# First loads of a two-layer decoder trunk: x and the first weight chunk on three queues instead of one

## The chip, the cores and the metric

The kernel runs on one core of a Trainium2 chip. The metric is the device time of one execution in microseconds (us); lower is better. The time before is 397.64 us, the median of three runs (397.17 to 398.45).

## What is computed

The reference is a decoder trunk of two layers on one sequence of 256 tokens with 1024 features. Layer 0 is a gated DeltaNet mixer, layer 1 a sparse-attention mixer. Only the head of layer 0 matters here: x is multiplied by a wide input matrix, whose columns give queries, keys, values, a gate and two small logits per head.

```python
def gated_deltanet_mixer(x, w_in, conv_w, a_log, dt_bias, norm_w, w_out):
    b_sz, t_len, _ = x.shape
    proj = x @ w_in
    qkv = jax.nn.silu(causal_short_conv(proj[..., :DN_QKV_WIDTH], conv_w))
    z = proj[..., DN_QKV_WIDTH:DN_QKV_WIDTH + DN_VAL_WIDTH]
    b_logit = proj[..., DN_QKV_WIDTH + DN_VAL_WIDTH:DN_QKV_WIDTH + DN_VAL_WIDTH + DN_HEADS]
    a_logit = proj[..., DN_QKV_WIDTH + DN_VAL_WIDTH + DN_HEADS:]
    ...
    return o.reshape(b_sz, t_len, DN_VAL_WIDTH) @ w_out
```

Everything else (the delta rule, the normalisation, the attention of layer 1, the output projections) comes after and is not touched.

## The kernel before

All arithmetic is in float32, and each large product is made of three matmuls: an operand is split into a high part, a cast to the type `fp32r`, and a low part, the difference to the original. For x these are `xh` and `xl`, for a weight chunk `hi` and `lo`. A product is high by high, low by high and high by low.

**Weights.** They stream from device memory in chunks of 128 x 1024 float32 (512 KB). `load_to` (line 156) issues the loads on the queue of the sync engine (SP) into a ring of five buffers named `raw`. `split_to` (lines 173 to 180) makes the high part on the scalar engine (ACT) and the low part on GpSimd (Pool); for the second chunk alone half of the cast and the low part are done on the vector engine (DVE). A `raw` buffer is free for another load when its low part is done. The order of chunks is the list `order`: 24 of `wqkv` first.

**The opening.** The transposed x, `xT`, is 128 x 8 x 256, 1 MB; it is loaded in four quarters of 256 KB (line 280), two of the eight blocks of 256 columns each. The first weight chunk, `first` (in the trace `raw_first`), is loaded in two halves of 256 KB (line 279). The tuple `FIRST = (1, 2)` puts a half ahead of the second and of the third quarter. All six are issued on SP's queue. The small logit matrix `wba` (64 KB) is loaded on ACT's queue (line 272), after a dummy exponential that brings in ACT's function table (line 269). Two small tables go out on Pool's queue, `sel` (line 288, 4.5 KB) and `nw` (line 290, 0.5 KB); `sel` is read first by `inv_expand`, some twenty chunks later, and `nw` later still.

Then ACT, DVE, Pool and the tensor engine (PE) work by quarters (the loop `for q in range(5)`). ACT casts, in this order: `wbs` from `wba` (line 308), the first quarter (line 333), the first weight half (line 316), the second quarter, the second weight half, and the last two quarters in four pieces. DVE makes `xl` from each (line 334), Pool `lo_first` from each weight half (line 317). PE runs 28 warm-up matmuls on a constant (line 324), then for each of the eight blocks four matmuls, two of the logits `gps` (line 338) and two of the first chunk `ps0` (line 340, `pv` in the trace), and two groups of four with the low weights (lines 343 and 352): 40 in all. The next chunk's matmuls (line 360) follow.

**What sets the order.** The order on PE, ACT, DVE and Pool is the order in which the program is written. SP's is left to a scheduler. Each load counts its completion on one of eight counters (`DMAHW0` to `DMAHW7`) for the queues of SP and ACT together, taken in turn, and on others (`DMASW`) for Pool's; the next load on a counter waits until the one before it has landed.

Of the kernel before, what the change touches and what calls it, by code (L numbers as in the profile page):

```python
# [9 lines left out]
F32 = mybir.dt.float32  # L10
F32R = mybir.dt.float32r
BF16 = mybir.dt.bfloat16
AF = mybir.ActivationFunctionType
# [4 lines left out]
P = 128  # L18
# [17 lines left out]
FIRST = (1, 2)  # L36
# [52 lines left out]
def trunk(ctx: ExitStack, tc: tile.TileContext, I: dict, out: bass.AP):  # L89
    nc = tc.nc  # L90
    V, S, G, PE = nc.vector, nc.scalar, nc.gpsimd, nc.tensor
# [22 lines left out]
    cp = ctx.enter_context(tc.tile_pool(name="cp", bufs=1))  # L114
# [14 lines left out]
    def xtile(tag, name, dt=F32R, shape=(P, 8, T)):  # L129
        return xp_.tile(list(shape), dt, tag=tag, name=name)  # L130
# [4 lines left out]
    def pjb(name):  # L135
        if state["wide"]:
            state["wide"] = 3 - state["wide"]
            if state["wide"] == 1:
# [4 lines left out]
    order = ([("wqkv", i) for i in range(24)] + [("wz", i) for i in range(8)] +  # L143
             [("wo", i) for i in range(8)] + [("skv", i) for i in range(4, 12)] +
             [("skv", i) for i in range(0, 4)] + [("bq", i) for i in range(4)] +
             [("w1", i) for i in range(4)] + [("bq", i) for i in range(4, 8)] +
             [("bz", i) for i in range(24)] + [("bo", i) for i in range(8)])
# [117 lines left out]
    warm = nc.const_aps.tensor(1.0, (P, 256), BF16)  # L265
    ones = cp.tile([P, 1], F32, name="ones")
    V.memset(ones, 1.0)
    tab = cp.tile([P, 1], F32, name="tab")
    S.activation(tab, ones, AF.Exp)
    xT = xtile("x1", "xT", F32)  # L270
    wba = cp.tile([P, 8, 16], F32, name="wba")
    nc.scalar.dma_start(wba, I["wba"])
    first = ring.tile([P, 1024], F32, tag="raw", name="raw_first", bufs=NRAW)
    raws[order[0]] = first
    state["l"] = 1
    for q in range(4):
        if q in FIRST:
            c = slice(FIRST.index(q) * 512, FIRST.index(q) * 512 + 512)
            nc.sync.dma_start(first[:, c], I[order[0][0]][0][:, c])
        nc.sync.dma_start(xT[:, 2 * q:2 * q + 2, :], I["xT"][:, 2 * q:2 * q + 2, :])  # L280
    al = cp.tile([P, 2, NH], F32, name="al")
    load_to(2)
    nc.sync.dma_start(al, I["al"].partition_broadcast(P))
# [1 line left out]
    nc.sync.dma_start(cw, I["cw"])  # L285
    load_to(3)
    sel = cp.tile([P, NSEL], F32, name="sel")
    nc.gpsimd.dma_start(sel, I["ca"])
    nw = cp.tile([P, 1], F32, name="nw")
    nc.gpsimd.dma_start(nw, I["nw"])  # L290
    ident, tri, suf = (cp.tile([P, P], F32, name=nm) for nm in ("ident", "tri", "suf"))
    for m, inc, base, cmp in ((ident, 1, 0, ALU.is_equal), (tri, 1, 0, ALU.is_ge), (suf, -1, 0, ALU.is_gt)):
        G.memset(m, 1.0)
# [10 lines left out]
    def add_pairs(n):  # L304
        G.tensor_tensor(pair[0:2 * n, 0:n], ident[0:2 * n, 0:n], ident[0:2 * n, n:2 * n], op=ALU.add)  # L305

    add_pairs(16)
    S.copy(wbs[:, :, 0:16], wba)
    V.tensor_tensor(wbs[:, :, 16:32], wba, wbs[:, :, 0:16].bitcast(F32), op=ALU.subtract)

    xh = xtile("xh", "xh")
    xl = xtile("xl", "xl")

    def split_first(c):
        h, l = splits[order[0]]
# [11 lines left out]
    for q in range(5):  # L327
        if q < 4:
            c = slice(2 * q, 2 * q + 2)
# [150 lines left out]
    def diag_ap(t):  # L480
        return bass.AP(tensor=t.tensor, offset=t.offset, ap=[[16 * 128 + 16, 128], [128, 16], [1, 16]])
# [77 lines left out]
        return MT1[r, h, c] if t == 0 else MT2[r, h, c]  # L559

    def inv_load():
        nc.sync.dma_start(Bd, diag_ap(scrM))

    def inv_rows(r):
# [111 lines left out]
    def clear():  # L676
# [4 lines left out]
        for t in range(2):  # L681
# [6 lines left out]
             6: [lambda: decay_rows(1), lambda: defer(1, lambda: decay_diff(1)), lambda: defer(1, lambda: decay_exp(0))],  # L688
             9: [lambda: defer(2, lambda: decay_exp(1)), lambda: clear()],
             INV + 1: [lambda: inv_load()],  # L690
             INV + 5: [lambda: inv_store()],
             INV + 7: [lambda: inv_expand()],
# [875 lines left out]
```

## Time and profile before

| | |
|---|---|
| time, median of 3 runs | 397.64 us (397.17 to 398.45) |
| the profiled execution's own time | 398.08 us |
| its span, first to last instruction | 396.1 us |
| mean granted clock of PE | 0.994 |
| PE busy | 383.1 us, 97% |
| ACT, DVE, Pool busy | 55%, 56%, 62% |
| loads and stores | 58.61 MB, mean 148 GB/s |

The page counts an engine as busy while any of its instructions runs. Matmuls overlap: one of 256 columns is shown as 0.28 us long while the next starts 0.12 us later, so a count of matmuls is turned into time with the pitch between starts, not with the length of one. "SPq", "ACTq" and "Pool" rows of the form `DMA_DIRECT2D` are the issue of a load, not its transfer; how long it takes to land is given by the view of the DMA issues. "Idle before <-releaser" in brackets is how long the engine stood idle, and what it was waiting for.

### The profile page before, as it was taken

How to read it: one execution, taken by the hardware profiler on the slowest of the kernel's cores; microseconds unless marked ns; L12 is line 12 of the kernel's file. 1: busy time of each engine (PE TensorE's matmuls, PEld its weight loads, DVE VectorE, ACT ScalarE, POOL GpSimd, SP SyncE). 2: the span in 40 equal slices, each digit the busy share in tenths (PEclk: the TensorE clock that was granted, in tenths of full speed). 3: DMA queues.
4: the chain of work that ended last, by engine and by line, in shares of the span. 5: the costliest groups of instructions: out<-in, count | busy, mean ns of one | idle time of the engine just before them, and what ended most of it. 6: DMA issues, size and time to landing. Idle time of an engine off the chain costs nothing.

```text
span 396.1 us, 7532 instructions
## 1 busy us (share of the span) xinstructions
PE 383.1 (97%) x2868; PEld 339.4 (86%) x2868; DVE 220.5 (56%) x583; ACT 218.6 (55%) x425; POOL 247.2 (62%) x158
## 2 busy tenths in 40 slices
PE   7999999999999999999999999999999999999992
PEld 4999999999989987868999888888888888778891
DVE  1778776668533455454530645645656465577626
ACT  4788666656654372625641658565474647456410
POOL 4699999747454856895872987193644637109051
PEclk9999999999999999999999999999999999999997
DMA  6866679744334314663554664243415243201011
GB/s 220 324 214 204 224 220 294 192 134 162 109 108 151 115 52 163 194 238 101 202 167 161 257 216 158 106 139 123 163 37 177 65 150 108 106 2 53 2 53 53
DMA packets 23475, 58.61 MB, mean 148 GB/s; under 512 B 6672, under 2 KB 9232, under 8 KB 23312
## 3 DMA queue, kind: packets, MB, share of 16 engines
q1 hardware_dynamic: 23232, 58.07, 44.2%
q8 instruction: 22, 0.36, 0.4%
q14 instruction: 13, 0.11, 0.1%
q10 hardware_dynamic: 144, 0.07, 0.1%
q0 software_dynamic: 64, 0.01, 0.0%
HBM read 55.90 MB, written 2.23 MB: 147 GB/s over the span
## 4 chain that ended last, share of the span: by engine, by line
PE 87%; POOL 4%; DVE 4%; DMA 2%; issue 1%; ACT 1%; POOLq 0%; SPq 0%; DVEq 0%; ACTq 0%
PE pbz L228 6%; PE pbz L230 5%; PE pbz L229 5%; PE op L1370 4%; PE s L1299 3%; PE ptp L1341 2%; POOL lo_skv L180 2%; PE pwz L228 2%; PE pk L210 2%; PE pbq L228 2%; PE pq L210 2%; PE pq L212 2%; PE pq L211 2%; PE pk L211 2%; PE pk L212 2%; PE pwz L230 2%
## 5 line engine op out<-in xcount | busy, mean ns | idle before, releaser
L180 POOL TENSOR_TENSOR lo_bz<-raw_bz,hi_bz 128x1024 fp32r<-128x1024 f32 x24 | 56.8, 2393 | 39.4 <-PE pbz L229 18.2
L180 POOL TENSOR_TENSOR lo_wqkv<-raw_wqkv,hi_wqkv 128x1024 fp32r<-128x1024 f32 x22 | 52.5, 2403 | 6.6 <-ACT hi_wqkv L176 4.5
L228 PE MATMUL pbz<-hi_bz,x1h 128*128 128x512 f32 x96 | 38.9, 405 | 0.0
L230 PE MATMUL pbz<-lo_bz,x1h 128*128 128x512 f32 x96 | 37.7, 392 | 0.0
L229 PE MATMUL pbz<-hi_bz,x1l 128*128 128x512 f32 x96 | 37.6, 392 | 0.0
L180 POOL TENSOR_TENSOR lo_bo<-raw_bo,hi_bo 128x1024 fp32r<-128x1024 f32 x8 | 18.9, 2388 | 23.7 <-ACT hi_bo L176 18.7
L180 POOL TENSOR_TENSOR lo_skv<-raw_skv,hi_skv 128x1024 fp32r<-128x1024 f32 x12 | 28.4, 2402 | 4.7 <-PE pskv L230 4.7
L180 POOL TENSOR_TENSOR lo_wz<-raw_wz,hi_wz 128x1024 fp32r<-128x1024 f32 x8 | 19.4, 2444 | 16.9 <-ACT hi_wz L176 16.9
L176 ACT CAST hi_bz<-raw_bz 128x1024 fp32r<-128x1024 f32 x24 | 25.2, 1052 | 4.1 <-POOL pair L305 2.7
L1348 ACT COPY PT<-ptp 128x512 f32<-128x512 f32 x24 | 14.1, 588 | 24.2 <-PE ptp L1341 24.2
L180 POOL TENSOR_TENSOR lo_bq<-raw_bq,hi_bq 128x1024 fp32r<-128x1024 f32 x8 | 19.1, 2397 | 12.6 <-ACT hi_bq L176 12.5
L180 POOL TENSOR_TENSOR lo_wo<-raw_wo,hi_wo 128x1024 fp32r<-128x1024 f32 x8 | 19.0, 2389 | 11.5 <-ACT hi_wo L176 11.5
L176 ACT CAST hi_wqkv<-raw_wqkv 128x1024 fp32r<-128x1024 f32 x22 | 22.8, 1043 | 0.8 <-DMA raw_wqkv<-in_wqkv 0.8
L228 PEld LDWEIGHTS pbz<-hi_bz,x1h 128*128 128x128 f32 x96 | 18.0, 188 | 4.1
L230 PEld LDWEIGHTS pbz<-lo_bz,x1h 128*128 128x128 f32 x96 | 18.0, 188 | 4.0
L229 PEld LDWEIGHTS pbz<-hi_bz,x1l 128*128 128x128 f32 x96 | 18.1, 188 | 2.8
L1332 ACT ACTIVATE pt<-s,mx 128x256 f32<-128x256 f32 x32 | 13.4, 472 | 11.0 <-DVE mx L1315 8.8
L210 PE MATMUL pk<-xh,hi_wqkv 128*128 128x256 f32 x64 | 18.7, 292 | 0.0
L210 PE MATMUL pq<-xh,hi_wqkv 128*128 128x256 f32 x64 | 18.5, 289 | 0.0
L212 PE MATMUL pq<-xh,lo_wqkv 128*128 128x256 f32 x64 | 18.1, 283 | 0.0
L211 PE MATMUL pq<-xl,hi_wqkv 128*128 128x256 f32 x64 | 18.1, 283 | 0.0
L211 PE MATMUL pk<-xl,hi_wqkv 128*128 128x256 f32 x64 | 18.1, 283 | 0.0
(357 smaller groups left out, 1259.1 us busy)
## 6 DMA issues: line engine op xcount, KB each, us to landing
raw_bz<-in_bz SPq DMA_DIRECT2D x24, 512.0 KB, 3.3
raw_wqkv<-in_wqkv SPq DMA_DIRECT2D x23, 512.0 KB, 4.2
raw_skv<-in_skv SPq DMA_DIRECT2D x12, 512.0 KB, 3.3
raw_wz<-in_wz SPq DMA_DIRECT2D x8, 512.0 KB, 3.8
raw_wo<-in_wo SPq DMA_DIRECT2D x8, 512.0 KB, 3.3
raw_bq<-in_bq SPq DMA_DIRECT2D x8, 512.0 KB, 3.5
raw_bo<-in_bo SPq DMA_DIRECT2D x8, 512.0 KB, 3.3
raw_w<-in_w SPq DMA_DIRECT2D x4, 512.0 KB, 3.5
```

The lines of the kernel that those rows point to most:

```text
L176: S.copy(h, r)
L180: e.tensor_tensor(l, r, h.bitcast(F32), op=ALU.subtract)
L210: PE.matmul(ps[:, 0:T], wh[:, kt, :], ah[:, kt, :], start=kt == 0, stop=False)
L211: PE.matmul(ps[:, 0:T], wh[:, kt, :], al_[:, kt, :], start=False, stop=False)
L212: PE.matmul(ps[:, 0:T], wl[:, kt, :], ah[:, kt, :], start=False, stop=kt == 7)
L228: PE.matmul(ps, ah[:, kt, tt], wh[:, k4, cols], start=kt == 0, stop=False)
L229: PE.matmul(ps, al_[:, kt, tt], wh[:, k4, cols], start=False, stop=False)
L230: PE.matmul(ps, ah[:, kt, tt], wl[:, k4, cols], start=False, stop=kt == 7)
L1299: PE.matmul(sp[:, j, 0:n], lq, kk[:, hh // 4, c0:c0 + n], start=i == 0, stop=i == 1)
L1332: S.activation(pt[:, :, b, :], s4[:, :, b, :], AF.Exp, bias=mx[:, b:b + 1])
L1348: S.copy(PT.rearrange("p a b c -> p (a b c)"), TP[u])
L1370: PE.matmul(o3[:, r, 1 + b, :], PT[:, j, b, :], vt_[:, b, j, g_, :], start=j == 0, stop=j == 1)
```

## The change

The six loads of the opening are divided among three queues. SP keeps the first and the third quarter of x. ACT's queue takes, after `wba`, the second quarter and the second weight half. Pool's queue takes the first weight half and the last quarter. The dummy exponential comes after ACT's three issues. `sel` and `nw` leave Pool's queue; they are written in `inv_load`, on SP's queue. The cast of `wba` is written after the allocation of `xh` and `xl` instead of ahead of it, with no other work between.

```diff
-    tab = cp.tile([P, 1], F32, name="tab")
-    S.activation(tab, ones, AF.Exp)
     xT = xtile("x1", "xT", F32)
     wba = cp.tile([P, 8, 16], F32, name="wba")
-    nc.scalar.dma_start(wba, I["wba"])
     first = ring.tile([P, 1024], F32, tag="raw", name="raw_first", bufs=NRAW)
     raws[order[0]] = first
     state["l"] = 1
-    for q in range(4):
-        if q in FIRST:
-            c = slice(FIRST.index(q) * 512, FIRST.index(q) * 512 + 512)
-            nc.sync.dma_start(first[:, c], I[order[0][0]][0][:, c])
-        nc.sync.dma_start(xT[:, 2 * q:2 * q + 2, :], I["xT"][:, 2 * q:2 * q + 2, :])
+
+    def load_x(e, q):
+        e.dma_start(xT[:, 2 * q:2 * q + 2, :], I["xT"][:, 2 * q:2 * q + 2, :])
+
+    def load_first(e, q):
+        c = slice(q * 512, q * 512 + 512)
+        e.dma_start(first[:, c], I[order[0][0]][0][:, c])
+
+
+    load_x(nc.sync, 0)
+    nc.scalar.dma_start(wba, I["wba"])
+    load_first(nc.gpsimd, 0)
+    load_x(nc.scalar, 1)
+    load_x(nc.sync, 2)
+    load_first(nc.scalar, 1)
+    load_x(nc.gpsimd, 3)
+    tab = cp.tile([P, 1], F32, name="tab")
+    S.activation(tab, ones, AF.Exp)
...
     sel = cp.tile([P, NSEL], F32, name="sel")
-    nc.gpsimd.dma_start(sel, I["ca"])
     nw = cp.tile([P, 1], F32, name="nw")
-    nc.gpsimd.dma_start(nw, I["nw"])
...
     def inv_load():
+        nc.sync.dma_start(sel, I["ca"])
+        nc.sync.dma_start(nw, I["nw"])
         nc.sync.dma_start(Bd, diag_ap(scrM))
```

Line numbers after `load_x` are higher in the changed kernel; the four casts of the opening are then lines 318, 340, 323 and 340.

The start of SP's queue before. `raw_wqkv_101` is the second weight chunk, `raw_wqkv_106` the third, 217, 219 and 221 the fourth to the sixth; `al` and `cw` are small tables, and the brackets name the counters and engines waited for:

```order
L280 DMA xT<-in_xT 128x512
L279 DMA raw_first<-in_wqkv 128x512
L280 DMA xT<-in_xT 128x512
L279 DMA raw_first<-in_wqkv 128x512
L280 DMA xT<-in_xT 128x512 x2
L156 DMA raw_wqkv_101<-in_wqkv 128x1024
L283 DMA al<-in_al 128x16 [waits DMAHW0_49]
L285 DMA cw<-in_cw 128x96 [waits DMAHW1_49]
L156 DMA raw_wqkv_106<-in_wqkv 128x1024 [waits DMAHW2_49]
L156 DMA raw_wqkv_217<-in_wqkv 128x1024 [waits DMAHW3_49]
L156 DMA raw_wqkv_219<-in_wqkv 128x1024 [waits DMAHW4_49]
L156 DMA raw_wqkv_221<-in_wqkv 128x1024 [waits DMAHW5_49,Pool_49]
```

The third chunk waits for counter 2, on which the second quarter of x lands. The same place after; here 215, 217 and 219 are the fourth to the sixth chunk, and `pek` and `pev` are two tables of 8 KB:

```order
L275 DMA xT<-in_xT 128x512 x2
L156 DMA raw_wqkv_101<-in_wqkv 128x1024
L293 DMA al<-in_al 128x16
L295 DMA cw<-in_cw 128x96
L156 DMA raw_wqkv_106<-in_wqkv 128x1024 [waits DMAHW0_49]
L156 DMA raw_wqkv_215<-in_wqkv 128x1024 [waits DMAHW1_49]
L156 DMA raw_wqkv_217<-in_wqkv 128x1024 [waits DMAHW2_49]
L569 DMA sel<-in_ca 128x9 [waits DMAHW3_49]
L570 DMA nw<-in_nw 128x1 [waits DMAHW4_49]
L1092 DMA pek<-in_pek 128x16 [waits DMAHW5_49]
L1092 DMA pev<-in_pev 128x16 [waits DMAHW6_49]
L156 DMA raw_wqkv_219<-in_wqkv 128x1024 [waits DMAHW7_49,DMASW0_49,Pool_49]
```

Four of the six x and weight loads have left the queue, the second chunk is its third load instead of its seventh, the third chunk waits for counter 0, on which ACT's `wba` lands, and `sel`, `nw`, `pek` and `pev` stand ahead of the sixth chunk.

The start of ACT's program before, from the table load to the last cast of x:

```order
L269 ACT_TABLE_LOAD
L269 ACTIVATE tab<-ones 128x1 [waits DVE_49]
L272 DMA wba<-in_wba 128x128
L308 CAST wbs<-wba 128x8x16 [waits DMAHW3_49]
L333 CAST xh<-xT 128x512 [waits DMAHW0_49]
L316 CAST hi_first<-raw_first 128x512 [waits DMAHW1_49]
L333 CAST xh<-xT 128x512 [waits DMAHW2_49]
L316 CAST hi_first<-raw_first 128x512 [waits DMAHW4_49]
L333 CAST xh<-xT 128x256 [waits DMAHW5_49]
```

And after:

```order
L283 DMA wba<-in_wba 128x128
L275 DMA xT<-in_xT 128x512
L279 DMA raw_first<-in_wqkv 128x512
L290 ACT_TABLE_LOAD
L290 ACTIVATE tab<-ones 128x1 [waits DVE_49]
L318 CAST wbs<-wba 128x8x16 [waits DMAHW0_49]
L340 CAST xh<-xT 128x512 [waits DMAHW1_49]
L323 CAST hi_first<-raw_first 128x512 [waits DMASW0_49]
L340 CAST xh<-xT 128x512 [waits DMAHW2_49]
L323 CAST hi_first<-raw_first 128x512 [waits DMAHW4_49]
L340 CAST xh<-xT 128x256 [waits DMAHW3_49]
```

Two more issues stand ahead of the table load, and the cast of the first weight half waits for a load of Pool's queue (`DMASW0`). The order of the casts is the same. On Pool, the issues of `raw_first` and `xT` stand where those of `sel` and `nw` stood.

## Rows read from the trace of the kernel before

**Rows 1.** The page's first part: busy us, share of the span, instructions.
```profile
PE 383.1 (97%) x2868; PEld 339.4 (86%) x2868; DVE 220.5 (56%) x583; ACT 218.6 (55%) x425; POOL 247.2 (62%) x158
```

**Rows 2.** Stretches: length, busy PE, PEld, DVE, ACT, POOL (instructions), clock, DMA share, GB/s.
```profile
6.30:14.00 7.70, 5.95 (x44) 4.98 (x44) 4.98 (x8) 4.48 (x9) 2.58 (x2) 1.00 0.95 350
14.00:380.00 366.00, 363.49 (x2735) 322.87 (x2733) 206.50 (x555) 211.47 (x412) 237.06 (x137) 1.00 0.45 147
```

**Rows 3.** The chain that ended last, 0 to 14 us: start, us, what.
```profile
1.71 6.79 DMA xT<-in_xT
8.52 0.63 ACT xh L333
...
13.34 0.47 PE pv L352 x4
```

**Rows 4.** Timeline of PE, 0 to 10 us: start, us, instruction [idle before].
```profile
0.84 5.50 PE L324 MATMUL warm<-const-bfloat16-1.0 128*128 128x256 bf16 x28 [0.84 <-PEq L1558]
...
6.86 0.38 PE L340 MATMUL pv<-xh,hi_first 128*128 128x256 f32 x1 [0.22 <-ACT hi_first L316]
...
9.19 0.31 PE L338 MATMUL gps<-xh,wbs 128*32 128x256 f32 x1 [1.23 <-ACT xh L333]
...
9.91 0.31 PE L338 MATMUL gps<-xl,wbs 128*32 128x256 f32 x1 [0.30 <-DVE xl L334]
```

**Rows 5.** Timeline of DVE, the last two subtracts of x.
```profile
11.38 0.75 DVE L334 TENSOR_TENSOR xl<-xT,xh 128x256 fp32r<-128x256 f32 x2
```

**Rows 6.** Timeline of SP's queue: issues of loads.
```profile
1.24 0.42 SPq L279 DMA_DIRECT2D raw_first<-in_wqkv  x1
...
2.65 0.91 SPq L280 DMA_DIRECT2D xT<-in_xT  x2
...
8.51 0.33 SPq L156 DMA_DIRECT2D raw_wqkv<-in_wqkv  x1
...
11.20 0.33 SPq L156 DMA_DIRECT2D raw_wqkv<-in_wqkv  x1
```

**Rows 7.** DMA issues at 1.24, 3.1 and 11.20: size, us from issue to landing.
```profile
raw_first<-in_wqkv SPq DMA_DIRECT2D x1, 256.0 KB, 4.9
...
xT<-in_xT SPq DMA_DIRECT2D x1, 256.0 KB, 7.4
...
raw_wqkv<-in_wqkv SPq DMA_DIRECT2D x1, 512.0 KB, 5.9
```

**Rows 8.** Stretches of half a microsecond, columns as in rows 2.
```profile
6.00:6.50 0.50, 0.50 (x5) 0.16 (x2) 0.27 (x2) 0.50 (x2) 0.00 (x0) 1.00 0.56 193
8.00:8.50 0.50, 0.00 (x0) 0.00 (x0) 0.00 (x0) 0.00 (x0) 0.17 (x1) 1.00 1.05 414
```

**Rows 9.** Timeline of ACT, 0 to 7 us.
```profile
0.80 1.28 ACT L269 ACT_TABLE_LOAD   x1 [0.80 <-PEq L1558]
...
5.47 0.30 ACT L308 CAST wbs<-wba 128x128 fp32r<-128x128 f32 x1 [3.17 <-DMA wba<-in_wba]
5.67 0.61 ACT L333 CAST xh<-xT 128x512 fp32r<-128x512 f32 x1
6.19 0.61 ACT L316 CAST hi_first<-raw_first 128x512 fp32r<-128x512 f32 x1
```

**Rows 10.** Timeline of POOL: its two issues, and its first weight subtracts.
```profile
1.31 0.78 POOL L288 DMA_DIRECT2D sel<-in_ca  x1 [0.81 <-POOLq L1558]
2.09 0.56 POOL L290 DMA_DIRECT2D nw<-in_nw  x1
...
14.38 9.48 POOL L180 TENSOR_TENSOR lo_wqkv<-raw_wqkv,hi_wqkv 128x1024 fp32r<-128x1024 f32 x4 [3.20 <-ACT hi_wqkv L176]
```

**Rows 11.** DMA issues on POOL's queue, and its packets from 4 to 5 us.
```profile
sel<-in_ca POOLq DMA_DIRECT2D x1, 4.5 KB, 5.0
nw<-in_nw POOLq DMA_DIRECT2D x1, 0.5 KB, 6.2
...
q0 software_dynamic: 17, 0.00, 5.6%
```

More of the change, by code (lines that the diff above doesn't have):

```diff
@@ L307, in trunk @@
     add_pairs(16)
+    xh = xtile("xh", "xh")
+    xl = xtile("xl", "xl")
     S.copy(wbs[:, :, 0:16], wba)
     V.tensor_tensor(wbs[:, :, 16:32], wba, wbs[:, :, 0:16].bitcast(F32), op=ALU.subtract)
-    xh = xtile("xh", "xh")
-    xl = xtile("xl", "xl")
     def split_first(c):
```

## The prediction

> **What bounds the kernel now.** The page's busy times come first: the tensor engine (PE) is busy for 383.1 of 396.1 us [rows 1]. A change that takes no matrix work away can win only where PE stands idle, so the next view is busy time by stretch. From 14 to 380 us PE is idle for 2.5 us in all (366.00 - 363.49) [rows 2]. The change touches none of that; it works on the opening, where PE runs 40 matmuls of real work (the row's 44, less the last warm-up matmul and three of the next chunk). The chain of waits gives their pitch, 0.47 us for four or 0.1175 each, and their end, 13.34 + 0.47 = 13.81 us [rows 3]. Forty of them need 4.7 us. The warm-up matmuls run from 0.84 to 6.34 [rows 4], so the opening takes 13.81 - 6.34 = 7.47 us, and **2.8 us of it are idle**. That is the most that this change can be worth.
>
> Who ends the idle time? The chain says: the load of the second quarter of x, issued at 1.71 and landing 6.79 later at 8.5; then its cast on ACT, its low half on DVE, and PE [rows 3]. PE waits 1.23 us for that cast; the waits behind DVE are short, such as the 0.30 at 9.91 [rows 4]. So the six loads of the opening set the time. All are on SP's queue today: quarter, weight half, quarter, weight half, quarter, quarter. The first weight half, issued at 1.24, landed 4.9 later, at 6.1; the last quarter, the second of the pair from 2.65 and so issued at about 3.1, landed 7.4 later, at 10.5 [rows 6, 7]. From the second quarter (8.5) to the last (10.5) three loads landed, 0.67 us each: that is the pace of one queue once it flows. Before that it did not flow: from 6.0 to 6.5 us the DMA engines were busy 56% at 193 GB/s, from 8.0 to 8.5 fully, at 414 GB/s [rows 8].
>
> **The change part by part.** *The split of the loads.* PE cannot start real work before 6.34, since the warm-up is kept, so the first quarter may land later than today by some tenths (its cast starts at 5.67 [rows 9]) at no cost. PE's second matmul needs the cast of the first weight half. That cast stands in ACT's row behind the first quarter's, and everything behind it on ACT waits with it. From its landing PE needs 0.65 us (0.61 for the cast [rows 9], and the start) and 39 matmuls, 4.6 us. So PE's opening ends no earlier than **landing + 5.25**. Today that floor is 6.1 + 5.25 = 11.4, and the late quarters of x add the other 2.4.
>
> After the change this half is the first load on Pool's queue, in the slot where the small table `sel` is today. That slot starts at 1.31 and takes 0.78 to issue [rows 10], and 4.5 KB issued there landed 5.0 later, at 6.3; the answers by microsecond show packets of its queue only from 4 us on [rows 11]. No row shows a large load on this queue. The bounds: not before 6.3, the landing of a table; not after 8.7, which is 1.31 plus 7.4, the slowest quarter of today. In between, 256 KB at the full pace add 0.67 to 6.3 (7.0), at a third of it 2.0 (8.3), since three queues then share the DMA engines. I take **7.5**, nearer the full pace, because the engines have idle room until 7 us.
>
> The Trainium skill (DMA: Bandwidth & Descriptors, Latency and other measured facts) gives a software-generated queue about 1 us to its first byte and a hardware one about 0.6. By that, an estimate from the page, the half would flow from about 2.5 us and be no later than today, worth some 2 us in the end. The trace disagrees: the packets of `sel` came at least 2.7 us after its issue began.
>
> The other loads: the second quarter becomes the second load of ACT's queue and the third quarter the second of SP's, the place from which the weight half landed at 6.1; with sharing I take 6.5 to 8. The second weight half is third on ACT's queue, as the second quarter is on SP's today (8.5). The last quarter is second on Pool's queue, where `nw` today lands at 2.09 + 6.2 = 8.3 [rows 10, 11]; with bulk in front and beside it I take 9.5 to 10.5, at worst as today. The ACT casts then run at 7.5, 8.0, 8.5 and so on, at the pitch of 0.52 of today's first two (6.19 - 5.67) [rows 9], and reach the last quarter at about 10. Even if it lands at 10.5, its two casts (0.7), DVE's last subtract (0.75 for two, so 0.4 [rows 5]) and six matmuls (0.7) end at 12.3. The weight half therefore rules: 7.5 + 5.25 = 12.75, and 0.2 for waits behind DVE like today's: **12.95 against 13.81, 0.9 us less**.
>
> *ACT's queue.* Two more issues, 0.4 us each by SP's [rows 6], now stand ahead of the table load of 1.28 and the dummy exponential. The table load starts near 2.1 and ends near 3.4, and ACT's next work stands at 5.47, where its small table lands [rows 9]: hidden with almost 2 us to spare. If that table came by 3.5, the 1.3 us would show.
>
> *Pool.* Two issues take the place of two issues; behind them come the masks, and then Pool waits for the cast of the weight half, as today. Nothing.
>
> *SP's queue.* Its order is not written by hand. The two small tables, with two others of 8 KB drawn forward, come to stand ahead of the sixth weight chunk: four issues, about 1.7 us. Today that chunk goes out at 11.20 and lands 5.9 later, at 17.1 [rows 6, 7]; its subtract is the last of the four that Pool runs from 14.38 in 9.48 us, so it starts at 21.5 [rows 10]. A delay of 1.7, and the cast between, fit there. Nothing on PE. In the other direction, the third chunk waits today for the second quarter of x and goes out at 8.51 [rows 6]; in the new order it waits for ACT's table and can go near 5.5. That is no gain, since PE does not wait for it, but it puts 512 KB more beside the last x loads; it is one reason why I leave the last quarter at up to 10.5.
>
> *After the opening.* Every engine's work hangs on PE's progress, and 2.5 us of idle time in 366 leave little that could swallow a shift, so I carry the 0.9 to the end in full. The sum is made against the profiled execution, 398.08, whose span is 396.1: 397.2. The median of the runs, 397.64, lies 0.44 below it, so the forecast is 397.64 - 0.9 = **396.7 us**.
>
> **The rivals.** *All loads come on time.* Three queues fill the idle room of [rows 8], and the weight half lands with the speed of a small table, at 6.3: PE ends at 6.3 + 5.25 + 0.2 = 11.75, a gain of 2.1, 395.6 us. For it: the engines' idle share, and loads that arrive more nearly in the order of use. Against it: that slot needs 5.0 us even for 4.5 KB.
>
> *Nothing moves.* The bytes are the same, the same DMA engines carry them, and the queues interleave: the weight half comes at 13.81 - 5.45 = 8.4 instead of 6.1 while the quarters come earlier, and PE ends where it did: 397.6. For it: from 8 us on the DMA engines are full [rows 8], and weight chunks now mix with the x loads. The Trainium skill has this as a rule (DMA: Bandwidth & Descriptors, Rules for kernel authors): spreading loads over several issuing engines does not help bandwidth and saves only issue time. The trace leaves room against it only in the first 7 us, where the engines were not full.
>
> *The Pool queue is late: slower.* The place is the cast of the first weight half; behind it wait all later casts of the opening, their subtracts on Pool and DVE, and 39 of the 40 matmuls. From 8.4 on, each microsecond costs one. If the half gets a quarter of the pace (6.3 + 4 x 0.67 = 9.0) and 0.7 of the hole that the second quarter shows today (8.5 - 6.1 - 0.67 = 1.7), it lands at 9.7, PE ends at 9.7 + 5.45 = 15.15, and the time is 397.64 + 1.3 = 399.0. For it: `nw`, 0.5 KB, took 6.2 us, longer than `sel` ahead of it [rows 11]. Against it: the DMA engines' room until 7 us.
>
> **How the numbers follow.** Forecast 0.42 (396.7), on time 0.27 (395.6), nothing moves 0.16 (397.6), Pool late 0.15 (399.0). A measurement of this kernel can tell about 0.3% from no change, 1.2 us: faster means under 396.45, slower over 398.83. Faster: 0.25 of the on-time case and 0.13 of the forecast's (weight half at 7.2 or sooner), 0.38. Slower: 0.13 of the late case and 0.02 of the unmoved one, 0.15. The rest, 0.47, is no difference. The range runs from 395.3 (the weight half at 6.2 and no wait behind DVE) to 398.8 (the weight half at 9.6); beyond it lie 0.13 of the late case and about 0.04 on the fast side.
>
> **What would show it.** PE's second real matmul (6.86 today [rows 4]) should stand near 8.1, and the wait of 1.23 at 9.19 should be gone; the next chunk's first matmul should stand near 12.95 instead of 13.81. Packets of Pool's queue should begin between 4 and 5 us. If the weight half lands before 7, the on-time case holds; after 8.4, the late one. The forecast is wrong in its base if the opening shortens and the span does not, since then something between 14 and 380 us takes the shift back.

## The result, and the profile after

The changed kernel takes 401.0 us (median of 7 runs, 399.17 to 402.28); the kernel before took 397.43 on the same chip (7 runs, 396.91 to 398.45). The ratio is 1.0082, with a 95% interval from 1.0065 to 1.01: it is slower, by 2.6 to 4.0 us. The forecast was 396.7 with a range up to 398.8, so it was wrong in sign and the range missed. The seven runs fall in two groups, 399.17 to 399.74 and 401.0 to 402.28, and the profile below is of the lower one.

The profiled execution took 399.74 (span 398.0). From 14 to 380 us PE was busy for 363.50 us, 363.49 before [rows 2], so in this execution nothing more is lost there. The difference lies in the opening. The chain of waits of the changed kernel at its start (start, us, what), and the view of its DMA issues from 0 to 12 us (size, us from issue to landing):

```profile
1.31 6.62 DMA raw_first<-in_wqkv
7.95 0.62 ACT hi_first L323
9.12 1.37 DVE xl L341
```

```profile
xT<-in_xT ACTq DMA_DIRECT2D x1, 256.0 KB, 5.1
raw_first<-in_wqkv POOLq DMA_DIRECT2D x1, 256.0 KB, 6.6
raw_first<-in_wqkv ACTq DMA_DIRECT2D x1, 256.0 KB, 8.1
xT<-in_xT POOLq DMA_DIRECT2D x1, 256.0 KB, 7.8
```

The chain now begins with Pool's load of the first weight half, not with the second quarter of x [rows 3]: the half landed at 1.31 + 6.62 = 7.93. The second quarter did come sooner, at 1.23 + 5.1 = 6.3 instead of 8.5, but had to wait in ACT's order behind the half's cast. The second weight half landed at 1.71 + 8.1 = 9.8 and the last quarter at 2.09 + 7.8 = 9.9. PE's timeline (start, us, instruction, idle before it), one row of the same timeline of the kernel before, and two stretches of the windows of the changed kernel (length, busy PE, PEld, DVE, ACT, POOL, granted clock, DMA share, GB/s):

```profile
8.62 0.38 PE L347 MATMUL pv<-xh,hi_first 128*128 128x256 f32 x1 [2.80 <-ACT hi_first L323]
...
9.66 0.28 PE L347 MATMUL pv<-xh,hi_first 128*128 128x256 f32 x1
10.54 0.42 PE L345 MATMUL gps<-xl,wbs 128*32 128x256 f32 x1 [0.60 <-DVE xl L341]
10.76 0.42 PE L347 MATMUL pv<-xl,hi_first 128*128 128x256 f32 x1
...
15.54 0.28 PE L367 MATMUL pv<-xh,hi_wqkv 128*128 128x256 f32 x1
```

```profile
13.65 0.28 PE L360 MATMUL pv<-xh,hi_wqkv 128*128 128x256 f32 x1
```

```profile
10.36:13.77 3.41, 3.23 (x16) 3.02 (x17) 3.03 (x7) 2.96 (x8) 1.29 (x2) 0.50 1.02 384
14.00:380.00 366.00, 363.50 (x2734) 322.87 (x2733) 205.08 (x555) 210.98 (x410) 235.84 (x136) 1.00 0.44 147
```

PE waits 2.80 us for the half instead of 1.23 for the second quarter [rows 4]. Then, from 10.36 to 13.77 us, the granted clock is 0.50 (1.2 GHz instead of 2.4), and 16 matmuls start 0.21 apart instead of 0.1175. The kernel before had 1.00 in both stretches of [rows 2]. The second chunk's first matmul starts at 15.54; before it started at 13.65. The difference, 1.89, is that of the spans, 398.0 - 396.1 = 1.9. (The prediction's 13.81 is the end of the last matmul of the opening in [rows 3], 0.16 later than the next one's start; all ends of the opening below are such starts. The 15.70 in the expectation of after_again is an end like 13.81.)

Who took the DMA engines? From 6 to 7 us the queues (q1 is SP's, q10 ACT's, q0 Pool's: packets, MB, share of 16 engines) and SP's issues:

```profile
q1 hardware_dynamic: 45, 0.18, 45.2%
q0 software_dynamic: 40, 0.13, 33.0%
q10 hardware_dynamic: 44, 0.09, 23.1%
```

```profile
1.71 0.42 SPq L156 DMA_DIRECT2D raw_wqkv<-in_wqkv  x1
...
4.64 2.00 SPq L156 DMA_DIRECT2D raw_wqkv<-in_wqkv  x3
```

At that time SP's two quarters of x have landed (5.9). Its 45% is almost all the second weight chunk (4 KB a packet), which PE first needs after 12 us; it gets twice the share of ACT's queue with the second half.

### The profile page after: what moved, and what is told of

It reads as the page before. It is cut to its first block, busy times and chain, and to the rows that moved or that the text cites. A ratio compares the mean times of both kernels' runs of the same rounds, so it can differ in the third digit from the quotient of the medians.

```text
span 398.0 us, 7531 instructions
## 1 busy us (share of the span) xinstructions
PE 383.3 (96%) x2868; PEld 340.3 (85%) x2868; DVE 219.3 (55%) x583; ACT 218.3 (55%) x425; POOL 248.0 (62%) x158
## 4 chain that ended last, share of the span: by engine, by line
PE 87%; POOL 4%; DVE 4%; DMA 2%; issue 1%; ACT 1%; POOLq 0%; DVEq 0%; ACTq 0%
PE pbz L228 6%; PE pbz L230 5%; PE pbz L229 5%; PE op L1379 4%; PE s L1308 3%; PE ptp L1350 2%; POOL lo_skv L180 2%; PE pwz L228 2%; PE pk L210 2%; PE pbq L228 2%; PE pq L210 2%; PE pq L212 2%; PE pq L211 2%; PE pk L211 2%; PE pk L212 2%; PE pwz L230 2%
## 5 line engine op out<-in xcount | busy, mean ns | idle before, releaser
L180 POOL TENSOR_TENSOR lo_wqkv<-raw_wqkv,hi_wqkv 128x1024 fp32r<-128x1024 f32 x22 | 53.4, 2437 | 7.1 <-ACT hi_wqkv L176 4.9
```

The costliest lines, as they stand in the source:

```text
L180: e.tensor_tensor(l, r, h.bitcast(F32), op=ALU.subtract)
```

## The experiments

**One measure for all of them.** The table gives, for each profiled execution, the start of the second chunk's first matmul (the opening's end), those waits of PE after it that the kernel before does not have, and the span less both. In each row the opening's end, the waits, the span and the rest are of the one execution that was profiled; the median is of all.

| kernel | opening ends | later waits | span | rest | median, us | ratio to before (95%) |
|---|---|---|---|---|---|---|
| before, first profile | 13.65 | | 396.1 | 382.5 | 397.43 | |
| before, second | 13.81 | | 396.3 | 382.5 | | |
| before, third | 12.68 | | 395.2 | 382.5 | 397.39 | 1.0006 (0.9995 to 1.0017) |
| changed | 15.54 | | 398.0 | 382.5 | 401.0 | 1.0082 (1.0065 to 1.01) |
| after_again | 15.73 | 1.29 | 399.6 | 382.6 | 401.1 | 1.0092 (1.007 to 1.0113) |
| e1_warm50 | 15.21 | 1.73 | 401.5 | 384.6 | 403.3 | 1.0129 (1.0076 to 1.0181) |
| e2_half_on_sp | 16.20 | 0.43 | 399.2 | 382.6 | 400.98 | 1.0083 (1.0056 to 1.0111) |
| e3_two_queues | 12.99 | | 395.3 | 382.3 | 397.13 | 0.9996 (0.9985 to 1.0006) |
| e5_half_on_pool | 13.00 | | 395.4 | 382.4 | 397.39 | 1.0001 (0.9992 to 1.0011) |
| e6_lo2_on_pool | 16.38 | | 398.9 | 382.5 | 399.74 | 1.0056 (1.0035 to 1.0076) |
| e7_warm50_lo2 | 14.83 | | 397.5 | 382.7 | 399.59 | 1.0055 (1.0037 to 1.0073) |
| e8_chunk2_held | 14.39 | | 396.8 | 382.4 | 398.87 | 1.004 (1.0027 to 1.0054) |
| e9_two_queues_held | 12.87 | 0.2 | 395.6 | 382.5 | 397.3 | 1.0003 (0.9994 to 1.0012) |
| e10_held_warm50 | 13.66 | 0.7 | 397.0 | 382.6 | 399.09 | 1.0049 (1.0033 to 1.0064) |
| e11_low_after_xl | 13.32 | | 395.5 | 382.2 | 397.38 | 1.0004 (0.9996 to 1.0013) |
| e12_one_on_pool | 15.01 | 1.23 | 400.1 | 383.9 | 400.45 | 1.0071 (1.0051 to 1.0092) |

The rest is 382.2 to 382.7 wherever the clock stayed up after the opening (in e1 and e12 it fell again there). So the opening's end, and what it sets off just behind it, decide the time of an execution.

**The kernel before, two more profiles.**

> The unchanged kernel before, profiled once more, because its first profiled execution (span 396.1) lay above its median and the two-queue kernel had the same time with an opening that ended at 12.99. If everything between 14 and 380 us costs the same in all of these kernels, an execution near 397.1 (span near 395.3) must show the first matmul of the second chunk near 13.0, not 13.81. If it stands at 13.8 with a span of 395.3, then the opening's end does not carry through to the end and the reading of all these kernels by their opening is wrong.

> The unchanged kernel before once more, for a profile of an execution nearer its median. Over all kernels profiled so far the span is 382.3 to 382.7 us longer than the time at which the second chunk's first matmul starts, once later waits are added (13.81 and 396.3, 12.99 and 395.3, 13.00 and 395.4, 14.83 and 397.5, 16.38 and 398.9). If that holds, an execution near 397.1 has this matmul near 12.9; if not, a part of the difference lies after the opening.

The second profile (398.22 us, a long execution again, so it did not test its expectation) ended its opening at 13.81, the third (397.05) at 12.68. Rows of the third, ACT's, DVE's and PE's timeline:

```profile
6.75 0.62 ACT L333 CAST xh<-xT 128x512 fp32r<-128x512 f32 x1 [0.15 <-DMA xT<-in_xT]
...
7.40 1.11 DVE L334 TENSOR_TENSOR xl<-xT,xh 128x512 fp32r<-128x512 f32 x1 [0.61 <-ACT xh L333]
...
8.56 0.30 PE L338 MATMUL gps<-xl,wbs 128*32 128x256 f32 x1 [0.59 <-DVE xl L334]
...
12.68 0.28 PE L360 MATMUL pv<-xh,hi_wqkv 128*128 128x256 f32 x1
```

In this execution, near the median, the second quarter is there at 6.75 and not at 8.5. The profile that the prediction was made on was one of the longer ones, and its late quarter is why. On one measure, its idle time was 13.65 - 6.34 - 4.7 = 2.6 us, and that of the third profile is 12.68 - 6.13 - 4.7 = 1.85 (6.13 is the first real matmul there). Here the subtract of DVE takes 1.11 us instead of 0.69 and PE waits 0.59 for it: with the second quarter early, DVE's subtract runs beside Pool's first one already in the kernel before.

**The changed kernel again, and two first suspects.** After_again is the unchanged changed kernel. In e1 the warm-up was lengthened, so that PE does not stand idle before the half:

```diff
-    for _ in range(2 * NWARM):
+    for _ in range(50):
```

> The changed kernel once more, as the yardstick on this chip. In its first profile PE's second real matmul waited 2.8 us for the cast of the first weight half, which landed on Pool's queue at 7.93; the granted clock was 0.50 from 10.36 to 13.77; PE's opening ended at 15.70. Theory A (the late half, and the clock that falls after PE's wait) and theory B (the loads of x and the weight chunks share the DMA engines, so the last x loads come late) both expect the same here: a half that lands at 7.5 to 9, a stretch of 0.50 clock of 3 to 4 us, and 2 to 4 us more than the kernel before.

> The changed kernel with 50 warm-up matmuls instead of 28, so that PE stays at work until the first weight half lands; nothing else is changed. Theory A: the clock stays at 1.00, 15 or 16 matmuls run at 0.12 instead of 0.21 apart, PE's opening ends near 14.2 instead of 15.7, and the time is 1.2 to 1.6 us under the changed kernel on the same chip, still not under the kernel before. Theory B: the opening is set by the last loads and the time is that of the changed kernel within 0.4 us.

After_again has the half's cast at 8.38, the clock at 0.50 from 10.25 to 13.66, and a loss that the first profile did not have. DVE's and Pool's timelines of the changed kernel's first profile, where the low part of the second chunk is on DVE and that of the third on Pool:

```profile
13.51 1.23 DVE L180 TENSOR_TENSOR lo_wqkv<-raw_wqkv,hi_wqkv 128x1024 fp32r<-128x1024 f32 x1
...
13.76 3.23 POOL L180 TENSOR_TENSOR lo_wqkv<-raw_wqkv,hi_wqkv 128x1024 fp32r<-128x1024 f32 x1 [1.97 <-ACT hi_wqkv L176]
```

The same in after_again, with PE behind it, and a row of the chain of waits that leads there:

```profile
14.27 2.40 POOL L180 TENSOR_TENSOR lo_wqkv<-raw_wqkv,hi_wqkv 128x1024 fp32r<-128x1024 f32 x1 [1.57 <-ACT hi_wqkv L176]
...
14.43 3.32 DVE L180 TENSOR_TENSOR lo_wqkv<-raw_wqkv,hi_wqkv 128x1024 fp32r<-128x1024 f32 x1
17.68 0.41 DVE L355 COPY ba<-gps 32x256 f32<-32x256 f32 x1
...
18.14 0.61 PE L370 MATMUL gps<-pair,ba 32*128 32x16 f32 x4 [1.29 <-DVE ba L355]
```

```profile
1.71 8.99 DMA raw_first<-in_wqkv
```

Whichever of the two starts second ends about when it would if it ran after the other: 14.27 + 2.40 + 1.23 = 17.9 for DVE (17.75 in the trace), 13.51 + 1.23 + 2.40 = 17.1 for Pool (16.99). The Trainium skill (SBUF — State Buffer, SBUF: two separate sides) says that such a pair holds a shared port one at a time, for a whole instruction; these rows agree. When DVE is second, the copy `ba` stands behind it and PE waits. The chain to this wait starts at the second weight half, which landed at 1.71 + 8.99 = 10.70 and made DVE late; in the first profile it had landed at 9.8.

In e1 the clock stayed at 1.00 through the opening, which ended at 15.21; then DVE's subtract took 3.23, PE waited 1.73 for `ba`, and the clock fell afterwards (PE's timeline and windows of e1):

```profile
15.21 0.28 PE L367 MATMUL pv<-xh,hi_wqkv 128*128 128x256 f32 x1
...
18.06 0.61 PE L370 MATMUL gps<-pair,ba 32*128 32x16 f32 x4 [1.73 <-DVE ba L355]
```

```profile
19.54:22.95 3.41, 3.41 (x18) 3.41 (x17) 2.85 (x16) 3.12 (x6) 3.04 (x2) 0.50 0.64 251
```

So e1's gain came back behind the opening, with more: 403.3. Neither expectation held. The one that took the clock for the rest of the loss had the opening's end near 14.2, but the second half, there at 10.74, kept it at 15.21, only 0.52 before after_again; and it did not have the collision behind. One of e1's four executions took 398.80 at a mean clock of 0.996 (the others 0.990 to 0.992); it was not profiled, so what it escaped is not shown.

**Without the collision.** In e6 the second chunk's low part also runs on Pool; e7 has the longer warm-up as well.

```diff
-            e = V if state["s"] <= NVEC + 1 else G
+            e = G
```

> The changed kernel with the low part of the second weight chunk computed on Pool, in series with that of the third, and not on DVE beside it. Theory C (the two subtracts slow one another, and the copy of the logits behind DVE's holds PE): DVE makes that copy at about 14.5 instead of 17.8, PE does not wait for it, the opening itself still ends at 15.2 to 16.0 with the clock at half before it; 399.2 to 400.0 where the changed kernel takes 401.0. Rival (PE's wait there is covered by the half clock or by the third chunk's load): the time stays at 400.6 to 401.4.

> The same with 50 instead of 28 warm-up matmuls, so that PE does not stand idle before the first weight half. If the loss of the changed kernel is the sum of a late half, the half clock that follows PE's wait, and the copy held up behind DVE's subtract, then the last two are gone here: clock 1.0 through the opening, its end near 15.2, no wait for the copy, 398.3 to 399.3. Rival (the clock falls because of the DMA traffic or at a fixed time, not because of PE's wait): 0.50 in 10 to 14 us again, and 399.7 to 401.

E6's 399.74 is as theory C had it. E7's 399.59 lies between its two expectations: the clock held, but the time hardly fell. In neither does PE wait for `ba`. The same stretch of e6 and of e7:

```profile
8.25:14.75 6.50, 5.75 (x27) 5.27 (x28) 4.00 (x6) 4.66 (x10) 3.30 (x3) 0.50 0.90 327
```

```profile
8.25:14.75 6.50, 5.00 (x39) 4.48 (x40) 4.33 (x7) 4.67 (x10) 3.23 (x3) 1.00 0.90 318
```

In e6's profile the clock was at 0.50 from 8.2 to 15.0, in e7 at 1.00 throughout, and the opening ended at 16.38 and 14.83. But these two profiles are the longest of e6's four executions (400.56) and the shortest of e7's (399.21), so the 1.55 between them is not what the clock is worth: the medians are 0.15 apart. In e7 the late loads and the waits behind DVE are left, and its opening still ends 2.15 us behind the 12.68 of before.

**Which load is late, and why.** First, the half alone goes to Pool's queue and the other five stay on SP's (e5, with the tables moved as in the change), against the change with the half on SP's queue and the third quarter on Pool's (e2):

```diff
-            nc.sync.dma_start(first[:, c], I[order[0][0]][0][:, c])
+            (nc.gpsimd if q == FIRST[0] else nc.sync).dma_start(first[:, c], I[order[0][0]][0][:, c])
```

```diff
-    load_first(nc.gpsimd, 0)
+    load_first(nc.sync, 0)
     load_x(nc.scalar, 1)
-    load_x(nc.sync, 2)
+    load_x(nc.gpsimd, 2)
```

> The kernel before with one load moved: the first weight half goes out on Pool's queue, in the slot of the small table; the other five stay on SP's queue in their order, and the two small tables go out later as in the change. Theory A (a load on Pool's queue is late in itself): the half lands at 7.5 to 8.5 although little else shares the DMA engines, its cast waits, and the opening ends 0 to 0.8 us later than before; 397.1 to 398.0, clock 1.0. Theory B (it was late in the change only because SP's weight chunks went out early and took the larger share): it lands at 6.3 to 7.0, the x quarters come 0.67 earlier than before, and the time is 396.2 to 396.8.

> The changed kernel with two loads exchanged: the first weight half on SP's queue, the third quarter of x on Pool's. Theory A: the half lands at 5.5 to 6.2, PE's second matmul does not wait for it, the clock stays at 1.00, and PE's opening ends at 12 to 12.8, limited by Pool's two quarters (near 8 and 10): 1 to 1.8 us under the kernel before. Theory B: Pool's quarters and the second weight half still come at 9.5 or later beside the weight chunks, the opening ends at 13.5 to 15, and the time is that of the kernel before or up to 1.2 us more.

ACT's and PE's timeline of e5, then of e2:

```profile
6.84 0.62 ACT L314 CAST hi_first<-raw_first 128x512 fp32r<-128x512 f32 x1 [1.39 <-DMA raw_first<-in_wqkv]
...
13.00 0.28 PE L358 MATMUL pv<-xh,hi_wqkv 128*128 128x256 f32 x1
```

```profile
10.22 0.62 ACT L323 CAST hi_first<-raw_first 128x512 fp32r<-128x512 f32 x1 [2.63 <-DMA raw_first<-in_wqkv]
...
12.52 0.40 PE L345 MATMUL gps<-xl,wbs 128*32 128x256 f32 x1 [0.91 <-DVE xl L341]
```

The half on Pool's queue alone is there at 6.84 and costs nothing (397.39): as theory B had the landing, and theory A the time. And the half at 6.45 on SP's queue does not save the change (400.98, more than either expectation allowed): the second half, third on ACT's queue, now lands at 10.2, PE waits 0.79 and 0.91, and the clock falls at 12.6. So it is not one load that is late. That whatever shares the engines with SP's chunks comes late is the next thing to test.

**No load on Pool's queue; and the chunks held back.** E3 keeps three quarters on SP and gives both halves and the last quarter to ACT. In e8 (the change) and e9 (e3) a memset of one column on DVE holds back the second and third weight chunk. Their issues, with those of `al` and `cw`, are also written later, behind the cast of `wba` (not shown). The second chunk goes out at 6.93 in e8 and at 8.47 in e9. The edit of e3, then that of the memset:

```diff
-    load_first(nc.gpsimd, 0)
-    load_x(nc.scalar, 1)
+    load_first(nc.scalar, 0)
+    load_x(nc.sync, 1)
+    load_first(nc.scalar, 1)
     load_x(nc.sync, 2)
-    load_first(nc.scalar, 1)
-    load_x(nc.gpsimd, 3)
+    load_x(nc.scalar, 3)
```

```diff
+            if state["l"] <= 2:
+                V.memset(t[:, 0:1], 0.0)
             nc.sync.dma_start(t, I[k[0]][k[1]])
```

> The changed kernel without Pool's queue: SP loads the first, second and third quarter, ACT both weight halves and then the last quarter. Theory A: no load waits for Pool's queue, the first half lands near 6, the clock stays at 1.00, PE's opening ends at 11.8 to 12.5, 1.3 to 2 us under the kernel before. Theory B: the bytes and the DMA engines are the same, the last quarter lands at 9.8 or later behind the second weight chunk's larger packets, and the time is within 0.8 us of the kernel before.

> The changed kernel with its six loads on three queues as they are, but the second and the third weight chunk held back: a one-column memset on DVE, behind the subtract of wbs, makes their loads wait until about 6 us instead of going out at 1.7 and 4.6. Theory D (the loads of the opening come late because the second chunk, let out as SP's third load, takes the larger share of the DMA engines from 4.5 us on): the first weight half lands at 6.5 to 7.2, the second half and the last quarter by 9.0, the clock stays at 1.0, the opening ends at 12.3 to 13.2, 396.4 to 397.4. Rival (three queues beside one another, Pool's above all, are slow whatever SP sends): the first half lands at 7.8 or later again, PE waits over 2 us, and the time is 399 or more.

> The six loads on SP's and ACT's queues only (as in the two-queue kernel, which took 397.13), with the second and the third weight chunk held back in the same way. If the early second chunk still costs the last x loads something there, the second weight half and the last quarter land 0.5 to 1.0 sooner (near 7.8 and 8.7), but PE is bound from 9.16 on by DVE's subtract of the second quarter, which runs beside Pool's and takes 1.36: the opening ends at 12.4 to 13.0, 396.6 to 397.2. If the second chunk then comes too late (over 12.3), PE waits for its cast and the time is 397.3 to 398.

E3 needs what the kernel before needs, as theory B had it, and in its profile the clock never fell: dividing the loads over SP's and ACT's queues neither costs nor gains anything. There the second chunk stands behind three quarters on the same queue. E9 gained nothing more. For e8, the queues from 6 to 7 us, ACT, PE and one window:

```profile
q10 hardware_dynamic: 93, 0.18, 51.4%
q0 software_dynamic: 35, 0.11, 28.2%
q1 hardware_dynamic: 102, 0.01, 8.0%
```

```profile
7.49 0.62 ACT L325 CAST hi_first<-raw_first 128x512 fp32r<-128x512 f32 x1 [2.17 <-DMA raw_first<-in_wqkv]
...
8.16 0.58 PE L349 MATMUL pv<-xh,hi_first 128*128 128x256 f32 x1 [2.07 <-ACT hi_first L325]
```

```profile
8.25:11.50 3.25, 3.25 (x15) 2.95 (x16) 2.84 (x3) 2.35 (x7) 2.89 (x2) 0.50 0.84 269
```

ACT's share doubles, the second half is there by 8.5 and the last quarter by 8.7. This is theory D for the loads behind the first, and it shows that the early chunk made them late. But the first half comes at 7.49, between the two expectations, PE waits 2.07 us, the clock falls, and the time is 398.87. **This is the prediction's own premise, the half at 7.5, and it is slower than before.**

**The premise without the clock's fall.** E10 is e8 with 50 warm-up matmuls.

> The kernel with three queues and the second and third weight chunk held back (398.87; PE waited 2.07 us for the first weight half, the clock stood at 0.50 from 8.1 to 11.5, the opening ended at 14.39), with 50 instead of 28 warm-up matmuls so that PE works on until about 7.7. If the fallen clock is the whole rest of the loss: clock 1.0 from 6 us on, the half cast at 7.5 again, the opening's end at 12.8 to 13.4, 397.1 to 397.9, not to be told from before. If the loads cost something else, or the clock falls later instead: 398.4 or more.

ACT's timeline, then PE's:

```profile
7.48 0.62 ACT L325 CAST hi_first<-raw_first 128x512 fp32r<-128x512 f32 x1 [1.44 <-DMA raw_first<-in_wqkv]
...
10.07 0.31 PE L347 MATMUL gps<-xl,wbs 128*32 128x256 f32 x1 [0.60 <-DVE xl L343]
...
13.66 0.28 PE L369 MATMUL pv<-xh,hi_wqkv 128*128 128x256 f32 x1
...
228.15 0.66 PE L1198 MATMUL qtp<-ident,hlq 128*128 128x128 f32 x4 [0.38 <-DVE kl L1165]
```

The expectation failed: 399.09, no better than e8. The clock stayed at 1.00, but the opening shortened by 0.73 only, because the wait behind DVE, which the slow clock had covered, came to light; it ended 0.26 past the expected range. In the profile, 0.7 more went later: 0.3 at 17.8, where the held third chunk came late (its cast starts at 14.21), and 0.4 at 228. The wait at 228 has a fellow of 0.3 in e1's profile and in no other; e1 has the longer warm-up too, but so has e7, so its cause is open.

**The subtracts that run together.** E11 is e3 with Pool's first subtract made to wait for DVE's second, by a copy of one column (the edit is shortened; the cast and the subtract of a weight half are now two functions, `cast_first` and `low_first`):

```diff
+                if q == FIRST[0]:
+                    G.tensor_copy(token, xl[:, 2, 0:1].bitcast(F32))
+                low_first(half)
```

> The two-queue kernel (397.13) with Pool's first subtract, lo_first, put behind DVE's subtract of the second quarter (a one-column copy of xl on Pool makes it wait). If the two slow one another: DVE's subtract takes 0.7 instead of 1.36, PE's wait of 0.59 at 9.16 is gone, the opening ends 0.4 to 0.6 sooner, near 12.4, 396.5 to 396.8. If DVE's 1.36 has another cause: unchanged there, and PE may wait for the low weights instead; 397.1 to 397.6.

In e3 DVE's subtract beside Pool's:

```profile
7.75 1.36 DVE L341 TENSOR_TENSOR xl<-xT,xh 128x512 fp32r<-128x512 f32 x1 [1.03 <-ACT xh L340]
```

In e11, DVE's row and two of PE's:

```profile
7.70 0.69 DVE L346 TENSOR_TENSOR xl<-xT,xh 128x512 fp32r<-128x512 f32 x1 [1.03 <-ACT xh L345]
...
9.94 0.74 PE L359 MATMUL pv<-xh,lo_first 128*128 128x256 f32 x4 [0.59 <-POOL lo_first L328]
...
13.32 0.28 PE L376 MATMUL pv<-xh,hi_wqkv 128*128 128x256 f32 x1
```

The cause of the 1.36 is shown: alone, the same subtract takes 0.69. The gain did not come: PE waits 0.59 for Pool's subtract instead, and 0.28 for a later one of DVE. The time is that of before (397.38).

**Is it the second load on Pool's queue?** In e5, with one load there, the first packets of q0 came at 3.75 to 4 us; in the eight profiles with two, between 4.5 and 5.25. E12 moves the last quarter from Pool's to ACT's queue.

> The changed kernel with the last quarter of x moved from Pool's queue to ACT's, as its fourth load: the first weight half is then the only load on Pool's queue, and the second weight chunk still goes out early on SP's. If the second load on Pool's queue delays the first: packets of that queue from 3.75 to 4 us, the half lands at 6.8 to 7.3 instead of 7.9 to 8.4, PE's wait for it is under 1.7 us and the clock stays at 1.0 until then; the second half still comes late (near 9.5) behind SP's chunk, and the time is 397.4 to 399. If the traffic beside it is the cause: packets from 4.7 on, landing near 8 again, 400 to 401.

Packets of q0 in e5 from 3.75 to 4 us, and in e12 from 4.75 to 5, the first stretches with any:

```profile
q0 software_dynamic: 4, 0.02, 15.9%
```

```profile
q0 software_dynamic: 7, 0.03, 45.0%
```

That theory fell: the half is alone on the queue, its packets begin at 4.75 all the same, and it lands at 8.3. The late start goes with large loads on ACT's queue (all kernels with it have them, e5 has not), but no run took only these away, so why Pool's queue starts up to a microsecond later stays open.

No kernel beat the one before; e3, e5, e9 and e11 are equal to it within 0.2%.

## Why the prediction was wrong, step by step

Three steps of the sum failed: the base, the weight half's landing, and the waits behind it, which were put at 0.2 us in all. In the first profile the forecast end of 12.95 becomes 15.54 by 0.45 for the landing, 0.56 more behind DVE, 1.47 for the clock and 0.1 for the first matmul after the wait; after_again adds 1.29 behind `ba`, which the sum did not have.

- **The base.** The idle 2.8 us and the end at 13.81 belong to an execution of 398.08. The prediction set the gain off against the median, 397.64, as if only a constant lay between. The third profile shows that the difference is the opening itself: 12.68 at 397.05. The prize was 1.85 us there. The 2.8 also takes the end of the last matmul (13.81) for the start of the next chunk's first, which was 13.65; from start to start it is 2.6.
- **The half's landing.** Taken 7.5 (bounds 6.3 and 8.7), measured 7.93 in the first profile and just before 8.38 in after_again. The bounds held; the choice near the full pace did not. The reason given, idle room until 7 us, was true of the kernel before; the change itself fills that room with the second chunk, issued at 1.71 instead of 3.60. E8 gives 7.5 with the chunk held back, e5 6.84.
- **The waits behind DVE.** Taken 0.2 "like today's". In the changed kernel the matmuls at 9.66 and 10.54 lie 0.88 apart instead of 0.12: 0.76. With the half and the second quarter cast one behind the other, DVE's subtract meets Pool's and takes 1.36 instead of 0.69. The third profile of before has this wait too (0.59 at 8.56); the one that the prediction read had lost it, since its second quarter was late. E10, with full clock and the cast at 7.48, ended at 13.66 = 7.48 + 5.25 + 0.93. So even with the half at 7.5 and the clock up, the rule ends where the first profile of before ended (13.65), and a microsecond after the third.
- **The clock.** There was no term for it. The 30 matmuls from 10.54 to 15.54 take 5.00 us instead of 30 x 0.1175 = 3.53, since some 16 of them start 0.21 apart: 1.47. The sum for the changed kernel then closes to 0.1: 7.95 + 5.25 + 0.76 + 1.47 = 15.43, measured 15.54. Three pairs differ in the longer warm-up (after_again and e1, e6 and e7, e8 and e10), and in each the clock holds through the opening with it and falls without. But 1.47 is not what a held clock gives back, since other waits stand behind it: e1 and e10 shortened the opening by 0.52 and 0.73, and the medians went from 401.1 to 403.3, from 399.74 to 399.59 and from 398.87 to 399.09. So the 1.47 is shown as a part of the profiled execution's sum; no run won it back.
- **The third chunk.** "No gain, since PE does not wait for it" was right about the gain and missed the price. The earlier chunk puts Pool's subtract beside DVE's, and 0.2 us decide which is first (DVE by 0.25 in the first profile, Pool by 0.16 in after_again). In after_again it costs 1.29, in the first profile nothing; after_again against the third profile of before is 15.73 - 12.68 + 1.29 = 4.3 of the spans' 4.4.
- **The second half and the last quarter.** Taken 8.5 and 9.5 to 10.5, measured 9.8 to 10.7 and 9.9 to 10.9. The half was 1.3 to 2.2 late and the quarter's upper bound was missed by 0.4. With the first half on time (e2), and in after_again and e1, the chain of waits starts at the second half, whose landing the prediction named but did not carry on to PE's end.
- **What was right.** The opening sets the time and the shift is carried to the end in full (the table's rest column). ACT's table load is hidden: it ends at 3.48, the next cast starts at 4.65. The two tables on SP's queue cost nothing: e9 has them ahead of its chunks, from 5.88 on, e3 behind several, at 16.60, and both take the time of before. The packets of Pool's queue began between 4 and 5 us, as said (4.75 to 5). The place of the "Pool queue is late" rival was right, too; its price of 1.3 and its turning point of 8.4 were not, as e8 is slower with the half at 7.5.
- **The rival from the notes.** The rule cited there, of the Trainium skill (DMA: Bandwidth & Descriptors, Rules for kernel authors), that spreading loads does not help, fits e3 and e5, at ratios of 0.9996 and 1.0001. For the change itself it is too kind: it came out slower.

## What to carry to other kernels

When loads are moved off a queue, ask what moves up in it: here the freed places went to a weight chunk wanted last, and it took the largest share of the engines just when the loads wanted first were under way. Price a longer wait of PE by the clock as well, and an earlier transfer by the instructions that it starts on the neighbouring engine. And check, with a second profile, whether the profiled execution lies at the median before its idle time is taken for the prize.

## What the hardware showed that was not expected

- The granted clock was at 0.50 (1.2 GHz) from 10.36 to 13.77 in the changed kernel, 10.25 to 13.66 in after_again, 19.54 to 22.95 in e1 and 8.2 to 15.0 in e6. It fell after waits of PE of 2.80, 1.97 and 1.73 us (e1), at the end of one of 2.07 (e8), after 0.79 and 0.91 close together (e2) and, in e12, after 1.23; up to 1.7 us lay between the wait and the fall. It did not fall after 1.69 (second profile of before), 1.53 (e5) and 1.29 (after_again's second wait). These rows give no rule for the length of wait.
- Two subtracts of DVE and Pool that overlap run nearly as if one after the other: 0.69 becomes 1.36, 1.23 becomes 3.23 to 3.44, and on Pool 2.40 becomes 3.23, at the cost of the one that starts second.
- A load issued on Pool's queue at 1.3 has its first packet 2.4 to 4 us later.
